# Token sums of the feed-forward made tile by tile, wide slices, separate buffers for the output weights, and the check for further expert blocks moved behind the last expert

## The chip, the core and the metric

The kernel runs on one core of a Trainium2 chip. The metric is the time of one execution on the device in microseconds (us); the median of three runs counts. The engines are named as in the profile: PE does matrix products (PEld its weight loads), DVE and ACT elementwise work, POOL (GpSimd) elementwise work and indirect transfers, and SP issues most transfers. They work side by side, each through its own queue in order, and wait for each other by semaphores.

## The reference

Two blocks follow one another on 1024 tokens of width 1024, all in float32. The first is a token mixer and then a mixture of experts:

```python
# 32 experts in 4 groups, 2 experts per token
y = (jax.nn.silu(xb @ w_gate[e]) * (xb @ w_up[e])) @ w_down[e]
out = jnp.zeros((T, D), tok.dtype).at[row_tok].add(ys.reshape(n_rows, D))
x = x + out;  x = rmsnorm(x, final_g)
```

The second block is attention, pooling and a gated feed-forward:

```python
g_a, g_b = jnp.split(jax.nn.sigmoid(gates + b_gate[l]), N_BRANCH, axis=-1)
mix = (g_a * y_a + g_b * y_b) @ w_o[l]
x = x + rms_norm(mix, norm_mix_post[l])
f = conv_gated_ffn(rms_norm(x, norm_ffn_pre[l]), w_up[l], conv_w[l], conv_b[l], w_down[l])
x = x + rms_norm(f, norm_ffn_post[l])

def conv_gated_ffn(x, w_up, conv_w, conv_b, w_down):
    hu = x @ w_up                                   # 1024 -> 2 * 2816
    hc = conv_b + conv_w[2] * hu + conv_w[1] * back(hu, 1) + conv_w[0] * back(hu, 2)
    val, gate = jnp.split(hc, 2, axis=-1)
    return (jax.nn.gelu(gate, approximate=True) * val) @ w_down
```

Here back(hu, n) stands for hu moved n tokens later, with zeros ahead.

## The kernel before

**Precision.** Every float32 operand of a large product is split in two (`split`, from L48): a rounded high part, cast on ACT (L51), and the rest, subtracted on DVE (L52). `mm3` (from L57) then does three products, high by high (L61), high by low (L62), low by high (L64).

**The experts** (`moe`). Experts are taken one after another, 96 tokens each, in an order that changes group at each step. One step of the loop makes gate and up products of expert e, transposes the rows of expert e + 1 (L990), and then makes the down product of expert e - 1 and adds its rows to x1d in memory with an indirect transfer (L1037). `Feed` streams the weights: 192 chunks of 1 MB (six per expert) through 15 slots; a slot is loaded again (L932) once its chunk has been split.

More than 96 tokens for one expert are dealt with by `overflow_blocks`. It computes how many further blocks there are, reads that number into registers on every engine (L1070) and runs a loop that many times (L1072). With the inputs used here the loop's body doesn't run. It stands behind expert 15 (`Feed.stop = 15`): there the loop doesn't prepare the next expert's rows, the last down product is made by itself, and every engine goes through this place before expert 16 starts. While the check is pending, one chunk (`Feed.hold`) isn't loaded, since its slot serves as scratch.

**The start of the second block** (`second`). SP loads two gains (gf at L1202, gp at L1204) and four weight tiles, ACT and DVE split the weights, and for each 128 tokens SP loads the rows from x1d (L1211), which are normed twice and transposed (L1168).

**The combined tile** (pool c4). For d = 0 to 7 the attention output is multiplied by its weights (two products of 4 x 3 steps, halves h of 512 tokens), scaled by the gate ga (L1421) and added to cb (L1422) into cs, one tile of 128 x 8 x 1024. POOL issues the loads of ga and cb. From d = 4 on, `out_weight` loads and splits two tiles of w_o per step; its raw tile comes from the pool ws, which the other weights use too, with two buffers.

**The output projection** (pool c5). For each of eight rows of 128 tokens, `rows` splits a slice of cs into yh and yl, PE makes pmix, the sum is normed (L1158 to L1160), added to xn (L1465), stored, normed again, and handed to `Ffn.take`, which transposes it (L1527). Tokens 0 to 511 go to X[1] and X[2] as split operands, tokens 512 to 1023 unsplit to b12 and b22 (L1533).

**The feed-forward** (`Ffn`). Both large products are made by a scheme with seven block products in place of eight (products 1 to 7, order 1, 2, 6, 5, 7, 3, 4), which needs sums of token blocks and of weight blocks. `begin` makes products 1 and 2 of the first pairs from X[1] and X[2]. `factors` makes the token sums: t1 = b12 - b11 for X[5], t2 = b22 - t1 for X[6], b22 - b12 for X[7], b22 for X[3], and b21 - t2 for X[4]; t2 lies in four buffers of pool fsn, which the copies of products (`snap`, L1624) use as well. It is advanced by next(T) between the products of the first pair. `pair` runs 22 times: seven dots of 12 products, sums in PSUM, and then the convolution of the values (va); the one of the gates (ga), the gelu and the product on POOL (L1694) follow in the next pair, with stores to the array ad. Convolution outputs are in tiles of 2 x 512 from a pool with four buffers.

**The down-projection** (`down`). 77 steps (7 products x 11 blocks of the inner width). `load(n)` brings a block of ad and none to two blocks of w_down (L1746), `make(n)` splits both operands into fd tiles, and PE makes 12 products. In step n, load(n + 2) and make(n + 1) are issued. Raw blocks lie in four buffers of pool fa, two for a step with three blocks. The convolution of the last gates stands ahead of all this.

The order of instructions on each engine is close to the program's, but not the same: a planner may place an instruction earlier when its operands are ready.

## Time and profile before

| | us |
|---|---|
| three runs: median (lowest to highest) | 2582.93 (2581.37 to 2587.81) |
| the profiled execution, its time | 2577.51 |
| the profiled execution, its span | 2575.7 |
| PE busy in the span | 2400.2 |
| DVE busy | 1770.6 |
| ACT busy | 1288.6 |
| POOL busy | 574.1 |

The span runs from the first to the last instruction; the time of the execution has 1.8 us around it. The granted clock of PE was 0.972 of full speed over the span. In the rows below, a line of a timeline starts with the time from the span's start and the duration; a bracket at its end gives how long the engine stood idle before the instruction and what ended that. In the table of stages PEclk is the granted clock, 1.00 for 2.4 GHz and 0.50 for 1.2 GHz, as a mean over the stage.

### The profile page before, as it was taken

How to read it: one execution, taken by the hardware profiler on the slowest of the kernel's cores; microseconds unless marked ns; L12 is line 12 of the kernel's file. 1: busy time of each engine (PE TensorE's matmuls, PEld its weight loads, DVE VectorE, ACT ScalarE, POOL GpSimd, SP SyncE). 2: the span in 40 equal slices, each digit the busy share in tenths (PEclk: the TensorE clock that was granted, in tenths of full speed). 3: DMA queues.
4: the chain of work that ended last, by engine and by line, in shares of the span. 5: the costliest groups of instructions: out<-in, count | busy, mean ns of one | idle time of the engine just before them, and what ended most of it. 6: DMA issues, size and time to landing. Idle time of an engine off the chain costs nothing.

```text
span 2575.7 us, 30732 instructions
## 1 busy us (share of the span) xinstructions
PE 2400.2 (93%) x11353; PEld 1881.6 (73%) x11353; DVE 1770.6 (69%) x2420; ACT 1288.6 (50%) x1702; POOL 574.1 (22%) x552
## 2 busy tenths in 40 slices
PE   8999787979999899996999999998969999998998
PEld 5887575867777577775888777776858888886786
DVE  5647777448999699986512665565578777776766
ACT  5322145337777577776312765672344444444443
POOL 0104453121222122213101011101103443442001
PEclk9999898989999899998999999999989999999999
DMA  6213555369999799975022111117212322326846
GB/s 231 95 66 98 204 160 192 123 231 354 372 371 368 258 387 372 364 284 188 29 79 90 58 41 52 60 55 248 91 51 90 115 99 94 111 98 203 266 152 205
DMA packets 121666, 451.16 MB, mean 175 GB/s; under 512 B 17510, under 2 KB 20520, under 8 KB 95658
## 3 DMA queue, kind: packets, MB, share of 16 engines
q1 hardware_dynamic: 87136, 346.94, 37.4%
q0 software_dynamic: 31776, 100.73, 12.0%
q10 hardware_dynamic: 2602, 1.51, 0.3%
q8 instruction: 90, 1.47, 0.2%
q14 instruction: 62, 0.51, 0.1%
HBM read 382.79 MB, written 74.71 MB: 178 GB/s over the span
## 4 chain that ended last, share of the span: by engine, by line
PE 50%; DVE 5%; ACT 4%; DMA 3%; issue 3%; POOL 1%; SPq 0%; DVEq 0%; POOLq 0%; ACTq 0%
PE proj L61 10%; PE proj L62 10%; PE proj L64 10%; DMA draw<-in_w_down 2%; PE pmix L61 1%; PE pmix L62 1%; PE w_up L62 1%; PE w_gate L62 1%; PE pmix L64 1%; PE w_gate L61 1%; PE yd L61 1%; PE w_gate L64 1%; PE yd L62 1%; PE w_up L61 1%; PE w_up L64 1%
## 5 line engine op out<-in xcount | busy, mean ns | idle before, releaser
L979 DVE TENSOR_TENSOR wlo<-raw,whi 128x2048 fp32r<-128x2048 f32 (+1 forms) x195 | 439.3, 2256 | 74.0 <-ACT whi L978 70.6
L978 ACT CAST whi<-raw 128x2048 fp32r<-128x2048 f32 (+1 forms) x195 | 365.6, 1878 | 109.0 <-PE w_up L64 36.1
L61 PE MATMUL proj<-hh,wthi 128*128 128x512 f32 (+1 forms) x576 | 214.2, 375 | 1.2 <-ACT wthi L51 0.9
L62 PE MATMUL proj<-hl,wthi 128*128 128x512 f32 (+1 forms) x576 | 215.0, 374 | 0.1
L64 PE MATMUL proj<-hh,wtlo 128*128 128x512 f32 (+1 forms) x576 | 214.3, 373 | 0.0
L1037 POOL DMA_INDIRECT x1d<-y,tab x32 | 91.2, 2851 | 267.9 <-ACT whi L978 253.7
L52 DVE TENSOR_TENSOR wtlo<-wraw,wthi 128x1024 fp32r<-128x1024 f32 (+1 forms) x44 | 49.3, 1125 | 124.8 <-ACT wthi L51 124.5
L62 PE MATMUL proj<-fdbl,fdah 128*128 128x512 f32 x308 | 122.5, 398 | 7.9 <-DVE fdbl L52 7.8
L1694 POOL TENSOR_TENSOR va<-va,ga 128x1024 f32<-128x1024 f32 x22 | 67.9, 3088 | 272.0 <-ACT ga L1693 272.0
L61 PE MATMUL proj<-fdbh,fdah 128*128 128x512 f32 x308 | 121.0, 393 | 5.2 <-ACT fdbh L51 2.7
L61 PEld LDWEIGHTS proj<-hh,wthi 128*128 128x128 f32 x576 | 108.3, 190 | 19.1 <-ACT wthi L51 1.3
L62 PEld LDWEIGHTS proj<-hl,wthi 128*128 128x128 f32 x576 | 108.7, 189 | 17.3 <-DVE hl L52 0.3
L64 PEld LDWEIGHTS proj<-hh,wtlo 128*128 128x128 f32 x576 | 108.7, 189 | 17.2
L64 PE MATMUL proj<-fdbh,fdal 128*128 128x512 f32 x308 | 121.1, 393 | 0.0
L61 PE MATMUL proj<-xh,wh 128*128 128x512 f32 x240 | 99.3, 415 | 8.8 <-DVE up L185 8.7
L61 PE MATMUL w_gate<-whi,xh 128*96 128x512 f32 x256 | 102.4, 400 | 1.9 <-ACT xh L51 1.8
L61 PE MATMUL yd<-whi,ah 128*96 128x512 f32 x256 | 102.4, 401 | 1.1 <-ACT y L1035 1.1
L62 PE MATMUL w_gate<-wlo,xh 128*96 128x512 f32 x256 | 102.5, 401 | 0.0
L62 PE MATMUL w_up<-wlo,xh 128*96 128x512 f32 x256 | 101.7, 397 | 0.8 <-DVE wlo L979 0.8
L62 PE MATMUL yd<-wlo,ah 128*96 128x512 f32 x256 | 102.1, 400 | 0.0
L51 ACT CAST fdah<-draw 128x512 fp32r<-128x512 f32 x77 | 47.8, 621 | 108.1 <-PE proj L62 56.9
L64 PE MATMUL w_gate<-whi,xl 128*96 128x512 f32 x256 | 101.8, 398 | 0.0
(537 smaller groups left out, 6725.0 us busy)
## 6 DMA issues: line engine op xcount, KB each, us to landing
raw<-in_w_gate SPq DMA_DIRECT2D x64, 1024.0 KB, 16.9
raw<-in_w_down SPq DMA_DIRECT2D x63, 1024.0 KB, 19.3
raw<-in_w_up SPq DMA_DIRECT2D x62, 1024.0 KB, 19.1
wraw<-in_w_up SPq DMA_DIRECT2D x44, 512.0 KB, 3.4
draw<-in_w_down SPq DMA_DIRECT2D x88, 256.0 KB, 3.8
draw<-ad SPq DMA_DIRECT2D x77, 256.0 KB, 2.9
wraw<-in_w_in SPq DMA_DIRECT2D x32, 512.0 KB, 3.6
ad<-as POOLq DMA_DIRECT2D x44, 256.0 KB, 2.3
```

What stands on the lines that cost most here:

```text
L51: nc.scalar.copy(hi, src)
L52: nc.vector.tensor_sub(lo, src, f32(hi))
L61: nc.tensor.matmul(outs[i], lhsT=wh, rhs=xh[i], start=start, stop=False, skip_group_check=onto)
L62: nc.tensor.matmul(outs[i], lhsT=wh, rhs=xl[i], start=False, stop=False, skip_group_check=onto)
L64: nc.tensor.matmul(outs[i], lhsT=wl, rhs=xh[i], start=False, stop=stop, skip_group_check=onto)
L978: g.nc.scalar.copy(hi[:, sl], raw[:, sl])
L979: eng.tensor_sub(lo[:, sl], raw[:, sl], f32(hi[:, sl]))
L1037: return nc.gpsimd.indirect_dma_start(out=g.x1d, out_offset=bass.IndirectOffsetOnAxis(ap=rows, axis=0), in_=y.rearrange("p a b -> p (a b)" ...
L1694: nc.gpsimd.tensor_mul(va, va, ga)
```

## The change

Four places are touched.

The check for further blocks stands behind expert 31 (`stop = NE - 1`); the loop runs through experts 0 to 31 without it.

In the combined stage, cs is two tiles, one per half of the tokens, from a pool that stays open to the end of the up-projection. w_o has its own three raw buffers; two of its tiles are loaded and split at d = 0, one each at d = 1 to 6. `rows(0)` follows half 0 of d = 7.

The token sums move into `take`: for a = 4 to 7 it makes the quarter of t1, t2, X[5] and b22 - b12 that belongs to its 128 tokens. X[5] and X[6] lie where cs was. Three quarters of X[6] are split in `later`, the last in the last `take`, which also makes the sums for X[4] (`four`). `begin` makes products 1 and 2 for both prepared pairs, the last `take` between them, with transposes into free halves of their banks. The copies of the first pair use the pool ft. b12, b22, the convolutions' outputs and the final output lie in tiles of 4 x 512 from a pool with two buffers (value and gate of a pair in one tile). xn has one buffer instead of two.

In the down-projection the last gates' convolution stands behind make(0), and their gelu and product behind make(1). Loads of w_down blocks are dealt out anew over products 6, 5 and 7, and from step DEEP = 10 on one more step is loaded ahead, with every third step's blocks in the pool ft.

```diff
@@ class Feed
-    stop = 15
+    stop = NE - 1
@@ def second, combined stage
-    cs = pcb.tile([P, 8, S], F32, name="cs")
+    cs = [pcb.tile([P, 8, 512], F32, name=f"cs{h}", tag=f"c{h}") for h in range(2)]
+    pyr = stc.enter_context(tpool(tc, name="yr", bufs=2, side="right"))
     def out_weight(k):
-        raw = g.ws.tile([P, D], F32, name="wraw")
+        raw = pwr.tile([P, D], F32, name="wor")
...
+            tpool(tc, name="wor2", bufs=3) as pwr, \
...
-                nc.vector.tensor_add(cs[:, d, sl], cb[:, sl], ga[:, sl])
-            if d >= 4:
-                for k in range(*((d-4)*8//(8-4), (d-4+1)*8//(8-4))):
+                nc.vector.tensor_add(cs[h][:, d], cb[:, sl], ga[:, sl])
+                if d == 7 and h == 0:
+                    nxt = rows(0)
+            if d < 7:
+                for k in range(d + (d > 0), d + 2):
                     out_weight(k)
@@ def second, output projection
-            xn = pr.tile([P, D], F32, name="xn")
+            xn = pr.tile([P, D], F32, name="xn", bufs=1)
...
             else:
+                F.later()
                 stc.close()
                 F.open()
...
-        F.begin()
-        F.take(*last)
+        F.begin(last)
@@ class Ffn
-        self.ph = st.enter_context(tpool(tc, name="fh", bufs=4))
+        self.ph = st.enter_context(tpool(tc, name="fh", bufs=2))
+        self.psn = st.enter_context(tpool(tc, name="fsn", bufs=4))
...
     def wide(self, name):
-        return self.ph.tile([P, 2, 512], F32, name=name, tag="h")
+        return self.ph.tile([P, 4, 512], F32, name=name, tag="h")
...
+        b11 = [f32(t[:, :, sl]) for t in self.X[1]]
+        hi, lo = [t[:, :, sl] for t in self.X[5]]
+        t1 = self.tmp.tile([P, 4, P], F32, name="t1", bufs=1)
+        t2 = self.psn.tile([P, 4, P], F32, name="sn")
+        self.t2.append(t2)
+        b12, b22 = self.b12[:, :, sl], self.b22[:, :, sl]
+        v.tensor_sub(t1, b12, b11[0])
+        v.tensor_sub(t1, t1, b11[1])
+        v.tensor_sub(t2, b22, t1)
+        if a == 7:
+            self.six(3)
+        nc.scalar.copy(hi, t1)
+        v.tensor_sub(lo, t1, f32(hi))
+        v.tensor_sub(b12, b22, b12)
+        if a == 7:
+            for i in range(4):
+                self.four(i)
...
+    def six(self, i):
+        sl = slice(i * P, i * P + P)
+        split(self.g.nc, *(t[:, :, sl] for t in self.X[6]), self.t2[i])
...
+    def four(self, i):
+        v = self.g.nc.vector
+        for t in self.X[2]:
+            b = f32(t[:, :, i * P:i * P + P])
+            if t is self.X[2][0]:
+                v.tensor_sub(self.t2[i], b, self.t2[i])
+            else:
+                v.tensor_add(self.t2[i], self.t2[i], b)
...
+    def later(self):
+        self.X[6] = self.half("c1")
+        for i in range(3):
+            self.six(i)
@@ Ffn.begin
-            Y, X = self.bank(), None
+            Y, X = self.bank(), self.bank()
             self.dot(Y[:, 0], f, 1, True)
+            self.dot(X[:, 0], f, 2, True)
+            self.ready.append((f, Y, X))
             if j == 0:
-                X = self.bank()
-                self.dot(X[:, 0], f, 2, True)
-            self.ready.append((f, Y, X))
+                self.take(*last, (Y[:, 1], X[:, 1]))
@@ Ffn.pair
+        early = (self.pt, "ft") if T else ()
-        p1 = self.snap(Y[:, 0])
+        p1 = self.snap(Y[:, 0], *early)
@@ Ffn.down
+        DEEP = 10
-        more = {..., 6: ((1, 1), (0, 1)), 5: ((1, 0),), 7: (), ...}
+        more = {..., 6: ((1, 1), (0, 1)), 5: ((1, 1), (0, 1)), 7: ((1, 0),), ...}
+        def third(i, m):
+            return i == 6 and m % 2 == 0 or i == 5 and m % 2 == 1
...
+                    pool, tag = (self.pt, "ft") if n % 3 == 2 and n > DEEP else (self.pa, "a")
...
         make(0)
+        ga = after[0]()
+        make(1)
+        after[1](ga)
...
-            load(n + 2)
-            make(n + 1)
+            for q in range(n + 2 + (n > DEEP - 2), n + 3 + (n >= DEEP - 2)):
+                load(q)
+            if n:
+                make(n + 1)
```

## Rows read from the trace of the kernel before

**Rows 1.** The page, busy time of each engine.

```profile
PE 2400.2 (93%) x11353; PEld 1881.6 (73%) x11353; DVE 1770.6 (69%) x2420; ACT 1288.6 (50%) x1702; POOL 574.1 (22%) x552
```

**Rows 2.** Who waited for whom, PE, whole span (us in total, times, longest).

```profile
PE proj L61 <- ACT sn L1624: 18.7, 1, 18.7
PE tpf L1168 <- DVE rs_v L70: 18.4, 1, 18.4
...
PE proj L62 <- DVE fdbl L52: 7.8, 7, 2.5
PE pmix L61 <- ACT yh L51: 7.7, 1, 7.7
```

**Rows 3.** Stages: length, busy PE, PEld, DVE, ACT, POOL, PEclk, DMA share, GB/s.

```profile
890.00:1140.00 250.00, 248.49 (x1164) 179.39 (x1163) 224.34 (x153) 189.46 (x154) 54.55 (x26) 1.00 1.01 369
...
1735.00:1786.00 51.00, 39.34 (x166) 31.55 (x165) 35.18 (x49) 13.99 (x18) 10.00 (x20) 0.93 0.82 289
1786.00:1882.00 96.00, 96.00 (x429) 77.04 (x428) 43.05 (x53) 28.50 (x51) 16.13 (x29) 0.99 0.25 93
1882.00:1924.00 42.00, 19.03 (x74) 14.31 (x73) 38.97 (x49) 21.72 (x33) 2.30 (x3) 0.73 0.15 53
1924.00:2336.00 412.00, 411.68 (x1794) 336.30 (x1793) 313.76 (x316) 183.90 (x212) 157.30 (x132) 1.00 0.29 100
2336.00:2420.00 84.00, 73.66 (x302) 57.66 (x301) 61.14 (x85) 38.45 (x68) 12.59 (x11) 0.96 0.74 244
```

**Rows 4.** Timeline of PE, transposes of expert rows around the check.

```profile
814.92 1.02 PE L990 MATMUL tp<-ident,xb 96*128 96x96 f32 x8
...
832.92 1.02 PE L990 MATMUL tp<-ident,xb 96*128 96x96 f32 x8
...
921.67 1.02 PE L990 MATMUL tp<-ident,xb 96*128 96x96 f32 x8
```

**Rows 5.** The chain of waits at the check, then SP's first issue after it.

```profile
867.00 5.08 DMA x1d<-y,tab
...
872.89 0.33 SPq L932 DMA_DIRECT2D raw<-in_w_down  x1
```

**Rows 6.** Timeline of SP at the end of the experts.

```profile
1137.04 0.33 SPq L1202 DMA_DIRECT2D gf<-in_final_g  x1
...
1137.89 28.83 SPq L1136 DMA_DIRECT2D wraw<-in_w_in  x4
1177.27 1.83 SPq L1211 DMA_DIRECT2D y<-x1d  x4
```

**Rows 7.** Landing of those four row loads; then of expert weights, 620:660 and 780:820.

```profile
DMA to landing us min/median/max: 3.8/5.0/6.2
...
DMA to landing us min/median/max: 10.1/11.0/11.7
...
DMA to landing us min/median/max: 18.4/19.2/20.5
```

**Rows 8.** Timelines of DVE, then PE, where the combined tile is finished.

```profile
1776.70 1.22 DVE L52 TENSOR_TENSOR ol<-wraw,oh 128x1024 fp32r<-128x1024 f32 x1 [2.52 <-ACT oh L51]
...
1783.67 0.69 DVE L1422 TENSOR_TENSOR cs<-cb,ga 128x512 f32<-128x512 f32 x1
...
1785.49 0.79 PE L61 MATMUL pmix<-oh,yh 128*128 128x512 f32 x1 [7.73 <-ACT yh L51]
```

**Rows 9.** Timelines of DVE, then ACT, at the turn into the feed-forward.

```profile
1892.26 1.28 DVE L1160 SCALAR_TENSOR_TENSOR t<-xn,rs_o,gr 128x1024 f32<-128x1024 f32 x1 [0.46 <-POOL rs_o L72]
...
1908.04 0.68 DVE L52 TENSOR_TENSOR fx6l<-sn,fx6h 128x512 fp32r<-128x512 f32 x1
...
1920.91 0.59 ACT L1624 COPY sn<-proj 128x512 f32<-128x512 f32 x1 [0.59 <-DVE fx4l L52]
```

**Rows 10.** Timelines of PE at the down-projection's start, then of ACT in the up-projection.

```profile
2339.05 0.73 PE L61 MATMUL proj<-fdbh,fdah 128*128 128x512 f32 x2 [2.37 <-ACT fdbh L51]
...
2278.42 1.21 ACT L1633 ACTIVATE va<-proj,cw 128x1024 f32<-128x1024 f32 x1 [1.42 <-DVE proj L1683]
```

More of the change, by code (lines that the diff above doesn't have):

```diff
@@ L1406, in out_weight, with rows @@
         split(nc, oh[k], ol[k], raw)
+    def rows(a):
+        yh = pyr.tile([P, 8, P], F32R, name="yh")
+        yl = pyr.tile([P, 8, P], F32R, name="yl")
+        split(nc, yh, yl, cs[a // 4][:, :, a % 4 * P:a % 4 * P + P])
+        return yh, yl
     with tpool(tc, name="c4", bufs=2) as pr, \
+            tpool(tc, name="wor2", bufs=3) as pwr, \
             tpool(tc, name="ps_4", bufs=4, space=PSUM) as ps:
@@ L1437, in second @@
         nc.gpsimd.dma_start(out=gr, in_=I["norm_ffn_pre"].to_broadcast([P, D]))
-        def rows(a):
-            ta = slice(a * P, a * P + P)
-            yh = pr.tile([P, 8, P], F32R, name="yh")
-            yl = pr.tile([P, 8, P], F32R, name="yl")
-            split(nc, yh, yl, cs[:, :, ta])
-            return yh, yl
         last = None
-        nxt = rows(0)
+        F.tmp = pr
         for a in range(8):
@@ L1514, in load, with half, take @@
             self.raws[j] = t
-    def take(self, a, x):
+    def half(self, tag):
+        t = self.pcb.tile([P, 2, 4, 512], F32R, name="f" + tag, tag=tag)
+        return [t[:, 0], t[:, 1]]
+    def take(self, a, x, tp=None):
         nc = self.g.nc
-        tp = self.bank("tpf")
+        v = nc.vector
+        if tp is None:
+            tp = self.bank("tpf")
+            tp = tp[:, 0], tp[:, 1]
         sl = slice(a % 4 * P, a % 4 * P + P)
         if a == 4:
-            self.b12 = [self.wide("b12") for _ in range(2)]
-            self.b22 = [self.wide("b22") for _ in range(2)]
+            self.b12, self.b22 = self.wide("b12"), self.wide("b22")
+            self.X[5] = self.half("c0")
+            self.t2 = []
         for h in range(2):
-            t = tp[:, h].rearrange("p (k n) -> p k n", k=4)
+            t = tp[h].rearrange("p (k n) -> p k n", k=4)
             for k in range(4):
@@ L1531, in take, with begin @@
             else:
-                for i, b in enumerate(self.b22 if h else self.b12):
-                    nc.scalar.copy(b[:, :, sl], t[:, 2 * i:2 * i + 2])
+                nc.scalar.copy((self.b22 if h else self.b12)[:, :, sl], t)
+        if a < 4:
+            return
+        b11 = [f32(t[:, :, sl]) for t in self.X[1]]
[30 more added lines that the diff above has]
+            self.six(i)
     def open(self):
         tc = self.g.tc
-        self.stx = ExitStack()
         self.pw = self.stx.enter_context(tpool(tc, name="fw", bufs=1, side="right"))
-    def begin(self):
+    def begin(self, last):
         self.ready = []
@@ L1566, in put @@
                 k = slice(2 * q, 2 * q + 2)
[L1567 to L1575 removed]
+                split(nc, *(t[:, k] for t in self.X[i]), x[:, k])
+        put(7, self.b12)
         yield
[L1577 removed]
+        put(3, self.b22)
         yield
[L1579 to L1588 removed]
+        for i in range(4):
+            sl = slice(i * P, i * P + P)
+            split(nc, *(t[:, :, sl] for t in self.X[4]), self.t2[i])
         yield
@@ L1608, in run @@
         f0 = self.ready[0][0]
-        next(T)
         f0.sums(0)
@@ L1617, in run, with snap @@
             self.pair(j, f, Y, X, T if j == 0 else None)
-        self.after[1](self.after[0]())
         self.stx.close()
-        self.down()
-    def snap(self, t, pool=None):
-        s = (pool or self.psn).tile([P, 512], F32, name="sn")
+        self.down(self.after)
+    def snap(self, t, pool=None, tag=""):
+        s = (pool or self.psn).tile([P, 512], F32, name="sn", tag=tag)
         self.g.nc.scalar.copy(s, t)
@@ L1630, in conv @@
         v = nc.vector
-        o = self.wide("va" if c < NF else "ga").rearrange("p a b -> p (a b)")
+        if c < NF:
+            self.vg = self.wide("vg")
+        o = self.vg[:, :2] if c < NF else self.vg[:, 2:]
+        o = o.rearrange("p a b -> p (a b)")
         src = src.rearrange("p a b -> p (a b)")
@@ L1668, in pair @@
         self.dot(X[:, 1], f, 5, True)
-        p5 = self.snap(X[:, 1])
-        if T:
-            next(T)
+        p5 = self.snap(X[:, 1], *early)
         ahead("sums", 10)
@@ L1719, in gated, with down @@
             keep(7, s3)
-    def down(self):
+    def down(self, after):
         g, nc = self.g, self.g.nc
@@ L1725, in down @@
         st = ExitStack()
+        self.pd = st.enter_context(tpool(tc, name="fd", bufs=1, side="right"))
         pt = st.enter_context(tpool(tc, name="ft", bufs=1, side="right"))
@@ L1740, in load @@
             i, m = steps[n]
-            src = [self.ad[i - 1, m]] + [wd[m, q, h] for q, h in more[i]]
+            src = [self.ad[i - 1, m]] + [wd[m, q, h] for q, h in more[i] if i not in (6, 5) or third(i, m)]
             r = []
@@ L1767, in make @@
                 v.tensor_sub(t[6], r[2], t[5])
-            elif i == 6:
+            elif third(i, m):
                 v.tensor_sub(t[7], r[1], r[2])
-            elif i == 5:
+            elif i == 7:
                 v.tensor_sub(t[4], r[1], t[6])
-        self.pd = st.enter_context(tpool(tc, name="fd", bufs=1, side="right"))
         for n in range(2):
```

51 lines of the change are left out of this document (15 added, 36 removed).

## The prediction, made before the changed kernel was run

> **What bounds the kernel now.** I read the page's busy times first: PE is busy 2400.2 of 2575.7 us [rows 1], so a change can only win back time in which PE waits or runs at the lower clock. The list of PE's waits over the whole span says where that is [rows 2], the table by stages how much lies in each stage [rows 3], and the timelines and the chain of waits what ended each wait [rows 4 to 6, 8 to 10].
>
> The reader should see in the stage table that the long stages have nothing to give. PE is busy 248.5 of 250.0 us in the experts' second half, 96.0 of 96.0 in the rows of the output projection and 411.7 of 412.0 in the up-projection [rows 3]. The idle time sits at seams, and the diff touches four of them: the check for further blocks, the stage that forms the combined tile (51.0 - 39.3 = 11.7 us idle), the turn into the feed-forward (42.0 - 19.0 = 23.0 us) and the start of the down-projection (84.0 - 73.7 = 10.3 us) [rows 3]. In the experts the DMA engines are also at a share of 1.01, 369 GB/s [rows 3]; that matters below.
>
> **Part A, the check behind expert 31.** Removed: the pause after expert 15. Expert rows are transposed every 832.92 - 814.92 = 18.00 us; the fourth set after 832.92 comes at 921.67 [rows 4]. Without the pause it would come at 832.92 + 72.00 = 904.92. So the pause costs **16.75 us**, idle time and lower clock together.
>
> Added: the same pause between the last expert and the second block. A wait for the last scatter stands there already: SP's loads of x1d are issued at 1177.27 behind it, and PE waits 18.4 us in one piece [rows 2, 6]. What is new is that everything behind the check stays behind it. SP went on behind it at 872.89, after a scatter that landed at 867.00 + 5.08 = 872.08 [rows 5]: 0.8 us. And six loads that SP now issues before or during the last experts, gf, gp and four weight tiles [rows 6], are in its queue ahead of the row loads, with the four splits on ACT and DVE. The four row loads were issued over about 1.5 us, the first landing after 3.8 and the last after 6.2 us [rows 7]: one more 512 KB load each (1.5 + 6.2 - 3.8) / 3 = 1.3 us. Six ahead make 7.8 us. DVE ends the last weight's split (a subtraction of 1.2 us [rows 8] behind a cast) about 1.0 us after the first row has landed. Sum 0.8 + 7.8 + 1.0 = 9.6 us, **net of A: -7.2 us**. Bounds: -16 if the row loads go first (only the 0.8 is left), 0 if each of the six takes twice the 1.3 and the splits follow in line.
>
> A's hidden side: without the pause the weight stream loses its time to catch up. Landing takes 11.0 us at 620 to 660 and 19.2 at 780 to 820 [rows 7], 0.051 us more per us. At 1123 that makes 19.2 + 323 x 0.051 = 36 us. Fifteen chunks of 3.0 us (18.00 / 6) stand between freeing a slot and needing it, 45 us. Nine are left, so I cost this at nothing; if the cover goes, PE falls to the stream's pace, at most 0.051 x 323 = 16 us.
>
> **Part B, the combined tile in halves, buffers of their own for w_o.** Now the eight w_o tiles share two raw buffers with the other weights and arrive last: DVE sits 2.52 us for one at 1774, then works without a gap until the last cs at 1783.67 + 0.69, and PE, done at 1777.8, waits 7.73 us for yh [rows 8]. After: the last w_o split belongs to d = 6, and the split of row 0 needs only half 0. PE makes half 1 of d = 7 meanwhile (12 products of 412.0 / 1794 = 0.23 us [rows 3], 2.8 us). Half 0 then needs two DVE steps of 0.69 [rows 8] and an ACT cast near 1 us (a copy of half the size takes 0.59 [rows 9]): PE could go on at once. DVE may still lag by a pair or two of such steps, 1.4 to 2.8 us. **-5 us**, bounds 0 and -8. The bytes stay the same, and the stage's DMA share is 0.82 already [rows 3], which is the case for 0. The Trainium skill, in "DMA: Bandwidth & Descriptors", section "Issuing engines are not separate DMA queues", says that transfers from any engine run on the same 16 DMA engines and interleave; by that, more buffers on SP bring the ga and cb loads from POOL no sooner, B would be 0 and the sum 5 us higher.
>
> **Part C, the token sums by tiles.** Now all sums come in begin's wake: the last normed row is written at 1892.26 + 1.28 = 1893.5, X6 is complete at 1908.7, but the first copy of a product waits for a buffer that the last sums (X4) release, at 1920.91; PE idles 18.7 us for it [rows 2, 9]. DVE is busy 39.0 of 42.0 us there [rows 3]. After: three quarters of the sums for X5 and X6 run under rows 4 to 7, where DVE is busy 43.1 of 96.0 us [rows 3]. That moves 3 x 5 steps of 0.68 us [rows 9] under that cover; without it they would return as 10 us. The first pair's copies use other buffers, so that wait is gone by construction.
>
> What is late next: from 1893.5, eight transposes (1.0 us [rows 4]), a copy (0.6 [rows 9]), three subtractions (2.0), a cast (0.6) and a subtraction (0.7) give X6 near 1898.4, about where PE's 48 prepared products end. Dot 6 thus starts 23 us before 1921.5 (1920.91 + 0.59 [rows 9]). Then DVE bounds: X5's and b12's last quarter 1.4, the X4 sums 5.4, X7 and X3 2.4 each, X4's low parts 2.7, sums for the next pair and two additions to products 4.1, in all 18.4 us, to 1917. Dot 4 can end at about 1920. It is the fifth dot from 1921.5 now, at 2.8 us each and 1.7 for the lower clock, 1937. That is -17; I keep 2 us for steps of the weights in between: **-15 us**. Bounds: -4 if X6 is made behind the other 18.4 us of DVE work, -23 if no wait is left.
>
> xn has one buffer instead of two: the next row's load waits for this row's norm. A load (3.8 us at its quickest [rows 7]) and four steps of at most 1.3 [rows 9] make some 9 us against 96.0 / 8 = 12.0 per row [rows 3]: covered by 3 us, otherwise 7 rows times the excess.
>
> **Part D, the start of the down-projection.** Now PE waits 2.37 us for the first cast, which stands behind the last gate convolution on ACT, and 7.8 us in seven waits for low parts, the largest 2.5 [rows 2, 10]. After: the first two steps' factors are made ahead of, or between, that convolution and its gelu. The first two waits go (4.8 us). From step 10 on a third buffer pair lets loads run three steps ahead, and three-load steps come in every second step of products 6 and 5 in place of each step of 6; by the code the w_down loads stay at 88. Three of the other five waits lie behind step 10. With some lower clock around the waits, **-8 us**, bounds -2 and -13.
>
> The wide slices hold the same bytes in two buffers as four did, with the same last reader; the second dot of pair 1 is hoisted already. I cost both at 0.
>
> **Sum**: -7.2 - 5 - 15 - 8 = -35. The profiled execution took 2577.51 us (span 2575.7), so it would take 2542. The median of the runs is 2582.93, 5.4 higher; on that scale I forecast **2548 us**.
>
> **The rivals.**
> 1. *The check costs as much at its new place.* For it: six loads and four splits leave their cover. Against: the wait for the last scatter stands there anyway. A = 0: 2555.
> 2. *DVE becomes the bound at the turn.* For it: 39.0 of 42.0 us busy [rows 3]. Against: a third of that work moves away. C = -6: 2557.
> 3. *The 16 DMA engines are the limit in B and D.* For it: shares of 0.82 and 0.74 in both stages [rows 3]. Against: neither is 1. B = 0, D = -4: 2557. The page named in part B would have it so.
> 4. *The other side: the merged slices slow the up-projection.* ACT's convolution of an even pair already waits 1.42 us at 2278.42 for the buffer or DVE before it [rows 10]. If value and gate in one tile add a wait, it is paid in each of 22 pairs. From 35 / 22 = 1.6 us of PE time a pair it decides; at 2 us it gives 2582.93 - 35 + 44 = 2592. Against: PE waits 0.3 us in 412 [rows 3], and a gate has until the pair after next.
>
> **How the numbers follow.** Forecast 0.56; rivals 0.12, 0.16, 0.09 and 0.04; 0.03 for more gain than forecast. 2548 is the likeliest. All four parts at their good bounds would give 2583 - 16 - 8 - 23 - 13 = 2523, at their bad ones 2583 - 6 = 2577; neither is likely in full, and rivals 1 to 3 together stand at 2573. The range is 2527 to 2571. About 0.3% (7.7 us) is what a measurement here tells from no change. Below 2575: 0.91; within: 0.05; above 2591: 0.04.
>
> **What would show it.** A: no gap near 860; behind the last expert the first row transposes about 9 us later after PE's last expert product than now. B: the wait of pmix for yh under 3 us. C: no wait for a copy at dot 6; DVE's X4 before the fifth dot. D: no wait over 1 us at the first two steps. Wrong would be: a starved expert in the second half, a row wait in the output projection, or any regular PE wait in the up-projection.

## The result, and the profile after

| us | before | after |
|---|---|---|
| median of the runs (lowest to highest) | 2583.01 (2581.37 to 2587.81), 4 runs | 2542.09 (2541.73 to 2543.16), 4 runs |
| the profiled execution | 2577.51 | 2541.87 |
| its span | 2575.7 | 2540.1 |
| granted clock over the span | 0.972 | 0.976 |

The ratio of the medians is 0.9843, 95% interval 0.983 to 0.9857. The prediction was 2548 us, range 2527 to 2571; its sum on the scale of the profiled execution was 2542. The two profiled executions differ by 35.6 us, the medians by 40.9, since the execution of before that was profiled lies 5.5 us under its median. What follows divides up the 35.6; no cut shows where the other 5.3 of the medians lie.

The starts and ends of PE's products in the timelines cut the span at the seams. The same cuts serve all experiments, so the table stands here once, a line for each kernel that ran, one trace each (the names are those of the experiments below). "Experts" runs from the first product of y to the last; "check" from there to the first product of the second block; "combined, rows" from the first product with the attention output to the first product of the feed-forward; "up" from there to the last product with up-projection weights; "down" from there to the last product with fd factors.

```
us             experts  check  (to attention out)  combined, rows    up     down
before          568.70  25.03        527.73            164.44      450.83  229.70
after           552.59  29.15        528.08            161.31      436.45  223.51
difference      -16.11  +4.12         +0.35             -3.13      -14.38   -6.19
part                A                                    B            C       D

after_again     552.58  29.18        527.06            159.26      434.79  224.55
stop15          568.77  24.06        528.02            158.13      436.47  224.34
before_stop31   552.67  29.22        528.48            165.03      451.13  233.01
rows_first      552.57  23.15        534.22            160.50      436.23  222.84
rows_two        552.63  29.30        527.27            157.89      436.25  224.33
wo_old          552.58  28.94        527.12            163.56      436.21  223.69
c4_three        552.60  29.11        527.69            156.54      436.25  224.51
c4_three_again  552.58  29.08        528.28            155.82      436.25  223.56
sums_late       552.71  29.16        527.44            157.21      436.60  223.84
sums_whole      552.68  28.74        527.55            160.15      446.09  223.90
fd_place        552.72  29.15        528.10            160.86      436.24  226.05
no_deep         552.70  29.07        527.28            161.77      433.05  227.05
```

The differences in the table add up to -35.3. Most cuts repeat within a microsecond in kernels that don't touch them. "Combined, rows" doesn't: it lies between 157.2 and 161.8 us (mean 159.9) in the eight runs whose combined stage is as changed. "Up" has two strays (434.79, 433.05); in the second, no_deep, PE has no wait ahead of dot 6. In "down" the last tenth of the products runs at a granted clock between 0.93 and 1.00 whatever the kernel, so for part D a second cut is used, at the 832nd of its 924 recorded products, counted from the last up-projection product: 205.7 us before, 199.0 after, and 197.4 to 199.4 (mean 198.5) in the ten runs that leave this stage as changed. The kernel before spreads as well: before_stop31, whose down-projection is the same, has 233.0 in the table and 208.1 at the second cut. Ahead of the table, up to the first product of y, lie 599.6 to 605.3 us in the fourteen traces, though no edit touches that part. So the cuts are compared here, and whole times stand beside them.

The page's busy times of the changed kernel answer to [rows 1]: PE is 5.6 us less busy, so the other 30 us are idle time.

```profile
PE 2394.6 (94%) x11353; PEld 1879.3 (74%) x11353; DVE 1772.9 (70%) x2428; ACT 1285.8 (51%) x1696; POOL 596.2 (23%) x552
```

PE's waits over the whole span, which answer to [rows 2] (us in total, times, longest):

```profile
PE tpf L1168 <- DVE y L1223: 25.4, 2, 23.5
...
PE proj L62 <- DVE fdbl L52: 4.7, 6, 1.5
```

The 7.8 us for low parts are now 4.7. The 18.7 for a product's copy are 2.2 and the 7.7 before pmix are 1.8, as brackets further down show. The wait for the first rows has grown from 18.4 to 23.5. The stages, shifted to where they lie now, answer to [rows 3]:

```profile
890.00:1120.00 230.00, 229.71 (x1074) 165.83 (x1073) 206.48 (x143) 174.45 (x142) 71.95 (x24) 1.00 1.01 363
1723.00:1773.00 50.00, 42.84 (x171) 33.68 (x169) 34.81 (x48) 14.30 (x18) 9.92 (x19) 0.90 0.65 234
1773.00:1868.00 95.00, 94.73 (x431) 78.04 (x432) 51.40 (x69) 30.25 (x50) 17.73 (x30) 0.98 0.28 104
1868.00:1906.00 38.00, 30.17 (x119) 23.56 (x118) 35.42 (x49) 22.60 (x33) 2.32 (x3) 0.87 0.20 72
1906.00:2303.00 397.00, 396.58 (x1730) 323.69 (x1729) 312.03 (x312) 180.95 (x212) 156.46 (x132) 1.00 0.31 104
2303.00:2390.00 87.00, 80.73 (x341) 64.07 (x340) 64.94 (x92) 38.18 (x68) 12.16 (x11) 0.98 0.78 254
```

Idle PE time is 50.0 - 42.8 = 7.2 us in the combined stage (11.7 before), 38.0 - 30.2 = 7.8 at the turn (23.0) and 87.0 - 80.7 = 6.3 at the start of the down-projection (10.3). The rows of the output projection (94.73 of 95.00) and the up-projection (396.58 of 397.00) have nothing idle, as before.

**Experts.** The timeline of PE answers to [rows 4]: four steps take 905.27 - 833.27 = 72.00 us, so the pause is gone and no step is late.

```profile
833.27 1.02 PE L990 MATMUL tp<-ident,xb 96*128 96x96 f32 x8
...
905.27 1.02 PE L990 MATMUL tp<-ident,xb 96*128 96x96 f32 x8
```

The weight stream has less in hand. Here is one chunk, by the lines of its source line and then ACT's timeline:

```profile
L932 SPq DMA_DIRECT2D raw<-in_w_up x1: 328/328/328, 1081.8 to 1081.8; - x1
...
DMA to landing us min/median/max: 26.1/26.1/26.1
```

```profile
1114.53 1.91 ACT L978 CAST whi<-raw 128x2048 fp32r<-128x2048 f32 x1 [0.27 <-PE w_gate L64]
```

It is issued at 1081.8, lands 26.1 us later at 1107.9, and ACT wants it at 1114.53: 6.6 us are left, the least of any chunk whose landing the trace shows. The prediction had 36 us to land and nine left of 45; here 32.7 us lie between issue and need.

**The start of the second block.** One row of the chain of waits (the last scatter of expert rows), then timelines of SP, ACT, DVE and PE, which answer to [rows 6]:

```profile
1154.20 5.13 DMA x1d<-y,tab
...
1122.06 0.33 SPq L1202 DMA_DIRECT2D gf<-in_final_g  x1
1122.44 0.42 SPq L1204 DMA_DIRECT2D gp<-in_norm_mix_pre  x1
1160.20 1.75 SPq L1136 DMA_DIRECT2D wraw<-in_w_in  x4
1162.00 3.06 SPq L1211 DMA_DIRECT2D y<-x1d  x4
...
1164.54 1.04 ACT L51 CAST wthi<-wraw 128x1024 fp32r<-128x1024 f32 x1 [11.38 <-DMA wraw<-in_w_in]
...
1168.43 1.04 ACT L51 CAST wthi<-wraw 128x1024 fp32r<-128x1024 f32 x1 [0.23 <-DMA wraw<-in_w_in]
1169.70 1.06 ACT L1216 ACTIVATE y<-y 128x1024 f32<-128x1024 f32 x1 [0.23 <-DMA y<-x1d]
...
1165.62 5.12 DVE L52 TENSOR_TENSOR wtlo<-wraw,wthi 128x1024 fp32r<-128x1024 f32 x4 [12.16 <-ACT wthi L51]
1170.65 1.22 DVE L1217 TENSOR_TENSOR hs<-y,gf 128x1024 f32<-128x1024 f32 x1
...
1176.20 1.97 PE L1168 MATMUL tpf<-ident,y 128*128 128x128 f32 x8 [23.53 <-DVE y L1223]
```

gf and gp are issued ahead of the check after all; four weight tiles, not six loads, stand between it and the rows. ACT's casts follow their landings 1.3 us apart, and the first row lands just behind the last cast. DVE isn't free then: it ends the last weight's subtraction at 1165.62 + 5.12 = 1170.74 and works on the row (L1217) only behind it.

**The combined tile**, timelines of DVE and then PE, answer to [rows 8]:

```profile
1741.35 1.29 DVE L1430 TENSOR_TENSOR ga<-proj,ga 128x512 f32<-128x512 f32 x2 [2.41 <-DMA ga<-gad]
...
1753.57 1.23 DVE L52 TENSOR_TENSOR ol<-wor,oh 128x1024 fp32r<-128x1024 f32 x1 [2.33 <-ACT oh L51]
...
1764.85 0.69 DVE L1430 TENSOR_TENSOR ga<-proj,ga 128x512 f32<-128x512 f32 x1 [2.73 <-DMA ga<-gad]
...
1773.27 0.51 PE L61 MATMUL pmix<-oh,yh 128*128 128x512 f32 x1 [1.82 <-DVE ga L1430]
```

DVE still waits three times, twice for a gate and once for a w_o tile.

**The turn**, timelines of PE, DVE, PE, DVE, ACT and PE, answers to [rows 9]:

```profile
1877.71 0.79 PE L64 MATMUL proj<-fx1h,fw1l 128*128 128x512 f32 x1 [3.87 <-DVE rs_v L70]
...
1876.44 1.22 DVE L52 TENSOR_TENSOR fw1l<-wraw,fw1h 128x1024 fp32r<-128x1024 f32 x1
...
1884.77 1.05 PE L1541 MATMUL proj<-ident,t 128*128 128x128 f32 x8
...
1890.63 0.68 DVE L52 TENSOR_TENSOR fc<-sn,fc 128x512 fp32r<-128x512 f32 x1
...
1891.96 0.57 ACT L1656 COPY sn<-proj 128x512 f32<-128x512 f32 x1
...
1892.58 0.50 PE L61 MATMUL proj<-fc,fw6h 128*128 128x512 f32 x1 [2.18 <-ACT sn L1656]
```

PE now waits in the middle of its prepared products, 3.87 us. What it takes up then is a product with the low part fw1l of a weight, which DVE, busy with the row's norm and the sums, makes only at 1876.44 to 1877.66; from 1877.6 to 1882.5 the granted clock is 0.50 (1.2 GHz). The kernel before has no such wait there. Row 7 is normed at 1880.07 (its last step on DVE starts at 1878.78 and takes 1.29). Its transposes stand behind prepared products in PE's order and start at 1884.77; X6 is complete at 1890.63 + 0.68 = 1891.31; the copy that dot 6 waits for stands behind X7's casts on ACT and starts at 1891.96. Dot 6 starts 1892.58 - 1871.21 = 21.4 us after the feed-forward's first product; before it was 1921.5 - 1885.63 = 35.9.

**The start of the down-projection**, timelines of ACT and then PE, answers to [rows 10]:

```profile
2300.25 0.62 ACT L51 CAST fdah<-draw 128x512 fp32r<-128x512 f32 x1
...
2338.78 0.49 PE L61 MATMUL proj<-fdbh,fdah 128*128 128x512 f32 x1 [1.42 <-ACT fdbh L51]
2340.72 0.79 PE L62 MATMUL proj<-fdbl,fdah 128*128 128x512 f32 x1 [1.45 <-DVE fdbl L52]
```

The first casts stand 7 us ahead of the first product; PE has no wait at the first two steps.

### The profile page after: what moved, and what is told of

Same layout as the page of the kernel before. It is cut to its first block, busy times and chain, and to the rows that moved or that the text cites. A ratio compares the mean times of both kernels' runs of the same rounds, so it can differ in the third digit from the quotient of the medians.

```text
span 2540.1 us, 30696 instructions
## 1 busy us (share of the span) xinstructions
PE 2394.6 (94%) x11353; PEld 1879.3 (74%) x11353; DVE 1772.9 (70%) x2428; ACT 1285.8 (51%) x1696; POOL 596.2 (23%) x552
## 4 chain that ended last, share of the span: by engine, by line
PE 68%; DVE 6%; ACT 4%; issue 3%; DMA 2%; POOL 1%; SPq 0%; DVEq 0%; POOLq 0%; ACTq 0%
PE proj L61 11%; PE proj L64 11%; PE proj L62 11%; PE w_up L62 2%; PE w_gate L62 2%; PE w_up L61 2%; PE w_up L64 2%; PE w_gate L64 2%; PE w_gate L61 2%; PE yd L61 2%; PE yd L62 2%; PE yd L64 2%; DMA draw<-in_w_down 1%; PE pmix L61 1%; PE pmix L62 1%
## 5 line engine op out<-in xcount | busy, mean ns | idle before, releaser
L1037 POOL DMA_INDIRECT x1d<-y,tab x32 | 105.9, 3311 | 229.6 <-ACT whi L978 188.4
L1729 POOL TENSOR_TENSOR vg<-vg 128x1024 f32<-128x1024 f32 x22 | 66.6, 3026 | 258.7 <-ACT vg L1728 258.7
L72 POOL TENSOR_TENSOR rs_o<-rs_v,mhalf 128x1 f32<-128x1 f32 x48 | 38.3, 798 | 269.6 <-DVE ssf L1847 179.5
L61 PE MATMUL w_up<-whi,xh 128*96 128x512 f32 x256 | 101.1, 395 | 0.0
L64 PE MATMUL w_up<-whi,xl 128*96 128x512 f32 x256 | 100.5, 392 | 0.0
## 6 DMA issues: line engine op xcount, KB each, us to landing
raw<-in_w_down SPq DMA_DIRECT2D x63, 1024.0 KB, 21.7
```

The lines of the kernel that those rows point to most:

```text
L61: nc.tensor.matmul(outs[i], lhsT=wh, rhs=xh[i], start=start, stop=False, skip_group_check=onto)
L64: nc.tensor.matmul(outs[i], lhsT=wl, rhs=xh[i], start=False, stop=stop, skip_group_check=onto)
L72: nc.gpsimd.tensor_tensor(o, v, g.mhalf if n == 1 else g.mhalf.to_broadcast([P, n]), op=ALU.pow)
L1037: return nc.gpsimd.indirect_dma_start(out=g.x1d, out_offset=bass.IndirectOffsetOnAxis(ap=rows, axis=0), in_=y.rearrange("p a b -> p (a b)" ...
L1729: nc.gpsimd.tensor_mul(va, va, ga)
```

## Experiments

Differences are to the changed kernel, by the cuts of the table, where nothing else is said. Part A comes first, then B, C and D.

**A alone undone, and A alone.**

```diff
-    stop = NE - 1          # after -> stop15
+    stop = 15
-    stop = 15              # before -> before_stop31
+    stop = NE - 1
```

> The changed kernel with part A alone undone: the check for further blocks stands behind expert 15 again. Reading of the two traces (the pause after expert 15 was worth 16 us, and the check costs some 4.5 us at its new place): slower than the changed kernel by 11 to 12 us, 2553 to 2554 us. The prediction's sum for A: slower by 7.2 us, 2549 us. Rival 1 (the check costs as much at its new place): no difference, 2542 us.

Measured: 2551.75 us, ratio to before 0.9887 (0.9863 to 0.991).

> The kernel before with part A alone: the check for further blocks behind expert 31. Reading of the traces (16 us saved behind expert 15, some 4.5 us paid behind expert 31): faster than before by 11 to 12 us, and the start of the first products of the second block earlier by as much. The prediction's sum: 7.2 us. Rival (in the changed kernel something else helped at that place): below 9 us.

Measured: 2572.00 us, ratio to before 0.9955 (0.9939 to 0.9971). In both directions the experts change by 16.0 to 16.2 us, and the check's new place costs 4.2 (in the kernel before) to 5.1 (in the changed one): A is worth **11.1 to 12.0 us** by the cuts of these four traces. The prediction's 7.2 and rival 1's 0 are outside. The whole times moved less than the 11 to 12 us that were expected: 9.8 us in the kernel before, interval 7.5 to 15.7, and 9.7 from the changed kernel's median to stop15's. That leaves out rival 1's 0 as well, and the 7.2 only just; the stages that no edit touches spread by some microseconds.

**Rows ahead of the weights**, all four, then two.

```diff
+    for a in range(4):     # rows_first; range(2) in rows_two
+        row_load(a)
     with tpool(tc, name="ws0r", bufs=4, side="right") as ws0r:
         wu = [weight_tile(g, wi[12 + q], pool=ws0, praw=ws0r) for q in range(4)]
```

> The changed kernel with SP's loads of the first four rows of x1d ahead of the four weight tiles of the second block. Theory (each 512 KB load that stands ahead of the rows behind the check costs them 1.3 us): the first row is transposed 4 to 5.5 us earlier, near 1171 us in place of 1176.2, and the time falls to 2537 us. Rival (the four splits on ACT and DVE, not the loads, set the start): the first products wait for the weights instead, and the gain is below 2 us.

Measured: 2542.59 us, ratio 0.9845 (0.9825 to 0.9865). PE's timeline, then windows (columns as in [rows 3]):

```profile
1174.90 1.97 PE L1168 MATMUL tpf<-ident,y 128*128 128x128 f32 x8 [16.99 <-DVE rs_v L70]
...
1183.44 0.58 PE L61 MATMUL proj<-hh,wthi 128*128 128x256 f32 x1 [0.85 <-ACT wthi L51]
1185.90 0.58 PE L62 MATMUL proj<-hl,wthi 128*128 128x256 f32 x1 [1.88 <-DVE hl L52]
...
1181.00:1187.00 6.00, 3.12 (x11) 2.18 (x10) 5.79 (x9) 6.00 (x9) 0.81 (x2) 0.50 0.78 293
1187.00:1193.00 6.00, 6.00 (x36) 6.00 (x36) 3.79 (x9) 4.42 (x9) 1.51 (x4) 0.64 0.52 192
```

The loads' price is as expected: the wait for the first transposes is 16.99 in place of 23.53 us. But the first products then wait for the weights' splits, 0.85 and 1.88 us, and the granted clock stays at 0.50 (1.2 GHz) up to 1187 and is 0.64 on average up to 1193. In the changed kernel it is 0.91 already from 1182 to 1188. "Check" falls by 6.0 us and the next cut grows by 6.1. The rival holds: nothing is gained.

> Two edits in stages that can be read apart. First, the loads of rows 0 and 1 of x1d ahead of the four weight tiles, those of rows 2 and 3 behind them; second, three buffers for the gates and cb in the stage of the combined tile. With four rows ahead the first transposes came 6.5 us earlier, but the products then waited for the weights' splits at the lower clock and the gain was gone. Theory A (it is the weights' lateness that spends it): with two rows ahead the first transposes come 4 to 5 us earlier and 1 to 3 us of it are left at the end of the rows. Theory B (PE's clock and DVE's work on the rows set that stage, whatever comes first): nothing is left. The second edit: 3 to 5 us at the end of the combined stage, as in its own run. In all 2535 to 2539 us.

Measured: 2541.95 us, above the 2535 to 2539 expected, ratio 0.9841 (0.9823 to 0.9858). "Check" is 29.30, nothing gained, theory B; the second edit shows in "combined, rows" alone (157.89). Timelines of ACT, then PE:

```profile
1173.35 1.03 ACT L51 CAST wthi<-wraw 128x1024 fp32r<-128x1024 f32 x1
...
1179.12 1.06 ACT L1227 ACTIVATE y<-hs 128x1024 f32<-128x1024 f32 x1
...
1184.71 1.97 PE L1168 MATMUL tpf<-ident,y 128*128 128x128 f32 x8 [7.78 <-DVE y L1232]
```

The four weight casts (1173.35 to 1179.22) now stand ahead of row 1's step L1227 in ACT's order. That step starts at 1179.12, though DVE had made its operand by 1171.83, and PE waits 7.78 us for the row's transposes. The Trainium skill says in "Perfetto Trace Analysis", section "Tensor Engine Instruction (MATMUL, LD_WEIGHTS)", that ACT and DVE are strict FIFO; this trace agrees. So four casts, four subtractions and two rows' norms have to be done between the check and the first products, and the order among them only chooses who waits.

**Three buffers for ga and cb.**

```diff
-    with tpool(tc, name="c4", bufs=2) as pr, \
+    with tpool(tc, name="c4", bufs=3) as pr, \
```

> The changed kernel with three buffers in place of two for the gates ga and for cb in the stage that forms the combined tile. Theory (part B gave less than its 5 us since a gate's load is issued only when the combined tile two steps before is done, and DVE then waits 2.4 and 2.7 us for it): both waits go, the first pmix product comes 3 to 5 us earlier, and the time falls by as much, to 2537 to 2539 us. Rival 3 of the prediction (the 16 DMA engines are the limit there): the loads land no sooner, DVE waits as long, no difference.

Measured: 2539.31 us, ratio 0.9836 (0.982 to 0.9853); "combined, rows" 156.54.

> The changed kernel once more, for the comparison with the next run on the same chip: 2540 to 2543 us.

> The changed kernel with three buffers for the gates and cb, once more. Theory (its own stage ended 3.2 to 4.8 us earlier): 3 to 5 us below the run before it. Rival (later stages give it back): below 1 us.

Measured, on one chip: 2542.48 us (2538.24 to 2543.20) and 2536.41 us (2535.12 to 2537.75), ratios to before 0.9839 (0.9823 to 0.9856) and 0.9822 (0.9807 to 0.9837). DVE's waits in the combined stage, of after_again and then of c4_three_again:

```profile
DVE ga L1430 <- DMA ga<-gad: 5.2, 3, 2.7
```

```profile
DVE ga L1430 <- PE proj L64: 3.7, 4, 1.3
```

The waits for gates are gone and DVE waits for PE. "Combined, rows" is 156.54, 155.82 and (rows_two) 157.89, mean 156.8, against 159.9: **3.1 us**. Of the 6.1 us between the medians that stage explains about half; of the 4.8 between the two traces 2.4 lie ahead of the first product of y, which the edit doesn't touch. c4_three is the fastest version that ran. The loads carry the same bytes and land in time once they are issued earlier, so the 16 DMA engines were not what held them: rival 3 falls for B. The rule of the Trainium skill that was weighed there ("DMA: Bandwidth & Descriptors", "Issuing engines are not separate DMA queues") may hold all the same; at a share of 0.65 it decides nothing.

**w_o as before**: two tiles at each of d = 4 to 7, through the raw buffers of the other weights.

```diff
-        raw = pwr.tile([P, D], F32, name="wor")
+        raw = g.ws.tile([P, D], F32, name="wraw")
-            if d < 7:
-                for k in range(d + (d > 0), d + 2):
+            if d >= 4:
+                for k in range(2 * d - 8, 2 * d - 6):
```

> The changed kernel with the w_o tiles loaded and split as before: two at each of the last four steps, through the two raw buffers that the other weights use; the combined tile stays in halves and row 0 is still split behind half 0 of the last step. The prediction's part B: slower by 3 to 5 us. Reading of the two traces (B gave 1 us up to the first pmix product and 3 us up to the last): slower by 1 to 3 us. Rival 3 (the DMA engines are the limit): no difference.

Measured: 2543.15 us, ratio 0.9858 (0.9839 to 0.9877). PE's timeline:

```profile
1773.39 0.76 PE L61 MATMUL pmix<-oh,yh 128*128 128x512 f32 x1 [8.29 <-DVE ga L1429]
```

The wait before pmix is back at 8.3 us, although row 0 is split early. Yet "combined, rows" is only 3.7 us above the mean of 159.9 (163.56): the products ahead of that wait end 56.8 us after the stage's first one, in the changed kernel 61.5. Own buffers move more than half of that wait into the products, where DVE now stands for gates and w_o tiles: 5.1 and 2.3 us in the changed kernel, 3.8 and 4.3 in wo_old. Whether the w_o loads, earlier now, delay the gates' loads, no run took apart. And 163.56 against 164.44 before leaves about 1 us, within the spread, for the tile in halves alone.

**The token sums, late in the code, then over whole tiles.** sums_late calls the four quarters behind the last row's transposes. sums_whole makes them over all 512 tokens:

```diff
-        if a < 4:
+        if a < 7:
             return
...
+        for k in range(4):
+            t1 = self.tmp.tile([P, 512], F32, name="t1", bufs=1)
+            v.tensor_sub(t1, b12[:, k], b11[0][:, k])
+            v.tensor_sub(t1, t1, b11[1][:, k])
+            v.tensor_sub(self.t2[k], b22[:, k], t1)
+            split(nc, *(t[:, k] for t in self.X[6]), self.t2[k])
+            split(nc, hi[:, k], lo[:, k], t1)
+            v.tensor_sub(b12[:, k], b22[:, k], b12[:, k])
```

> The changed kernel with the token sums made all together: the transposes and copies of rows 4 to 7 stay where they are, but t1, t2, X5, X6 and b22 - b12 of all four quarters are made behind the last row's transposes, with the sums for X4 behind them. Buffers stay as they are (the first pair's copies in their own). Theory of the prediction (three quarters of the sums, 10 us of DVE work, found cover under the rows): dot 6 of the first pair starts some 10 us later, 2552 us. Rival (the gain of the turn came from the copies' own buffers alone, the sums were not on the path): below 3 us, 2542 to 2545 us.

Measured: 2540.31 us, ratio 0.9838 (0.9818 to 0.9858); "up" 436.60, no change, and below the times of both theories. That didn't answer the question, as the group of the first subtraction shows (count, duration in ns, first and last start):

```profile
L1565 DVE TENSOR_TENSOR t<-b,fx1h x4: 683/686/687, 1844.5 to 1879.0; 128x512 f32<-128x512 f32 x4
```

The first quarter still runs at 1844.5, under the rows: the planner moved it there, because a quarter needs only its own row. Something else can be read from this run. Its dot 6 starts 1885.22 - 1869.25 = 16.0 us after the feed-forward's first product, 5.4 us sooner than in the changed kernel; the 3.87 us wait isn't there. Yet nothing is gained: PE waits 2.45 and 1.79 us for copies of products, and the granted clock is 0.80 from 1885.2 to 1893.5. An earlier dot 6 is not by itself an earlier end.

> The changed kernel with the token sums made over all 512 tokens at once, block by block of the width, so that none can start before the last row is transposed; memory, buffers of the first pair's copies and the order of its products stay. In the run that only moved the quarters behind the last row in the code, the planner made two of them under the rows anyway. Theory of the prediction (10 us of DVE work found cover under the rows): the last dot of the first pair ends some 8 to 11 us later, 2550 to 2553 us. Rival (the copies' own buffers made the gain): below 3 us, 2542 to 2545 us.

Measured: 2552.71 us, ratio 0.9887 (0.987 to 0.9904); "up" 446.09. Timelines of DVE (the first and the last step for X6) and PE:

```profile
1880.23 0.69 DVE L1555 TENSOR_TENSOR t<-b,fx1h 128x512 f32<-128x512 f32 x1
...
1898.88 0.70 DVE L52 TENSOR_TENSOR fc<-sn,fc 128x512 fp32r<-128x512 f32 x1
...
1900.86 0.80 PE L61 MATMUL proj<-fc,fw6h 128*128 128x512 f32 x1 [16.71 <-ACT sn L1641]
```

PE waits 16.71 us for dot 6, though the first pair's copies have their own buffers here too. The cover under the rows is worth **9.6 us** of C (by the medians of the same chip, 2552.71 - 2542.48 = 10.2). The rest (450.83 - 446.09 = **4.7 us**) is the buffers and the new order together.

**The place of the fd factors.** The diff does two things to the first steps: it writes the last convolution behind make(0), and it opens `self.pd` first, so that the fd tiles lie where X5 and X6 did, not where X5, X7 and X3 did as before. This run keeps the order of the code and takes back the place in memory.

```diff
-        self.pd = st.enter_context(tpool(tc, name="fd", bufs=1, side="right"))
         pt = st.enter_context(tpool(tc, name="ft", bufs=1, side="right"))
...
+        self.pd = st.enter_context(tpool(tc, name="fd", bufs=1, side="right"))
         for n in range(2):
             load(n)
```

> The changed kernel with the pool of the down-projection's split factors opened behind that of its sums, as before, so that these factors lie where X3, X4 and weights of the last pair lay and not where X5 and X6 did. The order of the code is left as changed: convolution of the last gates behind the first factors. Prediction's reading of part D (the place of that convolution in ACT's order made PE wait at the start): no difference. Rival, read from the trace after (factors could be made 7 us before the last product since X5 and X6 had been read; before, ACT stood idle 5.6 us with the loads there): the first two waits come back, 2.5 to 5 us slower, 2545 to 2547 us.

Measured: 2546.32 us, as the rival said, ratio 0.9864 (0.9848 to 0.9881); "down" 226.05. ACT in the kernel before, then ACT and PE in this one:

```profile
2334.78 1.21 ACT L1633 ACTIVATE va<-proj,cw 128x1024 f32<-128x1024 f32 x1 [5.64 <-DVE proj L1683]
```

```profile
2307.91 1.21 ACT L1668 ACTIVATE vg<-proj,cw 128x1024 f32<-128x1024 f32 x1 [5.64 <-DVE proj L1718]
2309.01 0.61 ACT L51 CAST fdah<-draw 128x512 fp32r<-128x512 f32 x1
...
2310.14 1.20 ACT L1668 ACTIVATE vg<-proj,cw 128x1024 f32<-128x1024 f32 x1
...
2313.00 0.50 PE L62 MATMUL proj<-fdbl,fdah 128*128 128x512 f32 x1 [1.98 <-DVE fdbl L52]
```

ACT stands idle for 5.64 us ahead of the value convolution, as before the change, and casts behind it; in the changed kernel the first casts (2300.25) stand ahead of both convolutions, whose first starts at 2306.50. So the place in memory is what lets them start early. The order of the code counts too: here the first step's casts come ahead of the gate convolution (2310.14), in the kernel before behind it, and PE waits 0.48 and 1.98 us in the first two steps where it waited 2.37 and 2.48. By this comparison of two traces about half of these waits went with the new order, the other half with the memory. At the second cut of "down" (200.8) the run is 2.3 us above the mean of 198.5: the memory of the fd tiles is worth about **2.3 us** of D, by one trace against ten that spread over 2.0 us.

**Loads two steps ahead only.**

```diff
-        DEEP = 10
+        DEEP = 1000
```

> The changed kernel with loads of the down-projection two steps ahead throughout, never three, and without the third pair of raw buffers; the new spread of the w_down loads over products 6, 5 and 7 stays. Prediction's part D (three of the seven waits went by the deeper loads, some 3 us): slower by 2 to 4 us, with PE waits for fd factors in products 6 and 5. Rival (the spread of the loads alone did it, or the DMA engines are the limit): below 1 us.

Measured: 2544.08 us, ratio 0.9851 (0.9835 to 0.9868); "down" 227.05, at the second cut 200.8, again 2.3 us above the mean. PE's timeline:

```profile
2347.45 0.50 PE L62 MATMUL proj<-fdbl,fdah 128*128 128x512 f32 x1 [2.68 <-DVE fdbl L52]
...
2379.75 0.79 PE L62 MATMUL proj<-fdbl,fdah 128*128 128x512 f32 x1 [3.15 <-DVE fdbl L52]
```

Two waits of 2.7 and 3.2 us for low parts stand in products 2 and 6, where the changed kernel's longest is 1.45. The deeper loads are worth about **2.3 us** of D, again by one trace. Both sizes are rough: PE's waits for fd factors add up to 6.9 us in fd_place and 7.3 in no_deep, to 4.8 to 7.0 in the ten runs, and to 10.5 and 13.2 in the two traces with the stage as before. The whole times agree in direction: on the same chip sums_late, whose cuts are those of the changed kernel, took 2540.31.

## Why the prediction was right, point by point

The sum was -35, the two traces differ by 35.6 and their cuts by 35.3, and the experiments show a gain at all four places. That the numbers meet this closely is luck: two terms were off in opposite directions, and the execution of before that was profiled is a quick one. By the medians the gain is 40.9, and the 2548 us that was forecast on their scale lies 5.9 above the 2542.09 measured.

- **A: -7.2 predicted, -11.1 to -12.0 measured by the cuts.** The pause was sized rightly (16.75; 16.1). The term that failed is the price behind expert 31: "Six ahead make 7.8 us ... Sum 0.8 + 7.8 + 1.0 = 9.6". The wait for the first rows grew by 23.5 - 18.4 = 5.1, where the sign named was 9. Two of the six loads are still issued ahead of the check; four cost 4 x 1.3 = 5.2. The 0.8 is there (the last scatter lands at 1154.20 + 5.13 = 1159.33, SP issues at 1160.20), and so is the 1.0 (DVE starts on the first row about 1 us behind ACT). What pays for them is a term that the prediction didn't have: the last scatter lands 5.1 us after its issue, in the kernel before 7.2, in stop15 6.3. Why it lands sooner there no run took apart. Nor was it foreseen that the loads' order doesn't set the end: putting the rows first takes 6 us off the wait and gives it back in the next 12.
- **A's hidden side held, with less in hand**: 6.6 us where nine were counted. Both of its numbers were off, landing (26.1, not 36) and the time between issue and need (32.7, not 45).
- **B: -5 predicted, -3.1 in this pair of traces**, -4.5 against the mean of the eight runs (159.9). The mechanism "the last w_o split belongs to d = 6" holds and the pmix wait is 1.8. What the prediction left out is that a gate's load is issued only when the tile two steps before is done; DVE waits 5.1 us for it, and a third buffer takes that away.
- **C: -15 predicted, -14.4 measured.** The cover was priced at 10 us and cost 9.6 when taken away. The steps between were wrong. X6 was to be ready 4.9 us after the last row's norm and came after 11.2, since the transposes queue behind prepared products on PE, which themselves wait 3.87 us for a weight's low part, and weights' sums stand between on DVE. Dot 6 started 14.5 us earlier, not 23, and the sign "no wait for a copy at dot 6" failed by 2.18 us. DVE was to set the end of the first pair; in the trace PE works without a wait from dot 6 on, so its late start sets it. sums_late fits a bound behind dot 6 (5.4 us sooner there, and no shorter), but PE's waits are for copies on ACT, and part is the clock. That DVE is the bound isn't shown, and the close number may be luck.
- **D: -8 predicted, -6.2 measured**, -6.7 at the second cut, and partly for a reason that was not seen. (Counted from before_stop31's trace it would be -9.6 at that cut.) The prediction had the first cast "behind the last gate convolution on ACT". That holds for half of the first waits: with the new order and the old place in memory (fd_place) they are 2.5 us in place of 4.9. The other half hung on the memory that the fd tiles take, which the prediction didn't look at; ACT was idle ahead of both convolutions. fd_place shows 2.3 us for that place, no_deep 2.3 for the deeper loads. What is left, 2 us in this pair of traces, falls to the new order, the new spread of the w_down loads and what goes with them, which were not tried alone. The count of waits was misread too: after the first two, six are left and not five, and five of them lie behind step 10, not three.
- **Rival 1** falls by both A runs; **rival 2** too, in its price: PE idles 7.8 us at the turn, not the 17 (23.0 - 6) that C = -6 would have left, though DVE is busy 35.4 of 38.0 us there and its queue is what makes X6 late; **rival 3** falls for B by c4_three; **rival 4**: PE waits 0.4 us in the up-projection's 397.
- xn's single buffer cost nothing: no wait stands in the rows of the output projection.

## What to carry to other kernels

Price a moved wait by what still stands behind it in each queue, and by what no longer runs beside it; then try whether taking one load out of its way moves the end or only the next wait. When an engine stands idle with its inputs in place, ask what last read the memory it will write before blaming the order of its queue. Work that is cut along the rows as they arrive hides under them by itself; the same work over the whole tile cost 9.6 us here.

## What the runs showed of the hardware

Starting PE earlier with pauses between its first products was worth nothing: with the rows first it made its first transposes 6.5 us sooner after the experts, but waited in between, and 6 to 12 us after them the granted clock was still 0.50, in the changed kernel 0.91. And the landing times of the weight stream, at a DMA share of 1.01 without a break, stopped growing: 19.2 us at 780 to 820 in the kernel before [rows 7], then in the changed one 25.8 to 27.4 at 1000 to 1010, 26.1 at 1082 (where the earlier growth would have given 34), and 21.7 at 1105 to 1113.
